# A two-layer hybrid mixer step: GpSimd's element-wise work given to VectorE, and a list schedule made in rounds

## The chip, the core and the metric

The kernel runs on one core of a Trainium2 chip. A core has five engines that run side by side: TensorE (PE, matrix products into PSUM), VectorE (DVE, element-wise work and reductions), ScalarE (ACT, activations and copies), GpSimd (POOL, element-wise work on SBUF here) and SyncE (SP), which in this kernel issues all DMA transfers. Each engine takes its instructions in order; between engines they wait on semaphores. The metric is the device time of one execution in microseconds. TensorE's clock is granted by the chip, at 2.4 GHz or 1.2 GHz; profile rows give the granted share.

## What is computed

Two layers with separate weights run over 128 prompt tokens and 512 latent tokens (640 together, width 1024). In each layer:

```python
mod = silu(cvec) @ w_mod + b_mod                    # shift, scale, gate
h = rms_norm(x, g_pre) * (1 + scale) + shift
p = h @ w_in                                        # 1024 x 3456
ya = rwkv_branch(...)   # 4 heads of 64, two directions, state scan:
                        # s = s*w + (s @ -kk)(kk*a) + v k ; y = s @ r
yb = window_gqa(...)    # 2-D rope, windowed attention with a sink
yc = rglru_branch(...)  # conv over 4 taps, gated linear recurrence, two directions
yd = diff_attend(...)   # two softmaxes, p1 - lam * p2, 4 heads
y = concat(ya*silu(ag), yb*silu(bg), yc*silu(cg), yd*silu(dg)) @ w_out
x = x + gate * rms_norm(y, g_post)
```

The outputs are both token sets after two layers and the prompt's keys, values and final states.

## The kernel before

Tokens are held as five tiles of 128 (four latent, one prompt). Activations for products are kept as a high and a low part in single-pass float32 (tiles HA and HB), and weights are split the same way, so one projection step is three products (high x high, high x low, low x high). `split` (L519 to L525) makes the high part by a copy (ScalarE, or the engine called `self.G`, L524) and the low part by a subtraction (L525, `self.V` or `self.G`). All matrix products go through one helper, so they carry line L352.

A layer runs like this. Weights come in 512 KB pieces through two `raw` buffers (L536; modulation weights L420), are split into WP or WQ, and feed the input projection: feature-major tiles (`fm`) and token-major chunks (`tm_chunk`). Token-major chunks 2 and 4 get rotary embedding in `rope` (L586 to L591), five small element-wise instructions a tile, on `self.G`; chunks 0 and 1 on `self.V`.

The recurrence branch `lru` (L1002) is a convolution, gates, and scans; its tables LRU_CONV, LRU_Q, LRU_U, LRU_S, LRU_H say which steps use `self.G` (1) or `self.V` (0). `stt` (L990) does a step as one scalar-tensor-tensor instruction on VectorE or as two instructions on `self.G`.

The RWKV branch is blocked: chunks of 64 tokens, and for each of two directions d the stages pre (decays and scaled keys), mats (masked block products, L1210), ends, inv, keys, solve; then a chain over chunks, a readout, and the normalisation `rwkv_out`. `rwkv_inv` (L1251) inverts 80 triangular 32x32 blocks at once: the blocks go through DRAM into a layout with one block a partition (L1262, L1264), then for each of 31 columns j an outer product (L1278) and a subtraction (L1280) of j(32-j) elements. CUT = 24 divides the columns: for direction 0 GpSimd has columns below 24 and VectorE the last 8, for direction 1 the mirror. The result goes back through DRAM (L1282, L1283, then four L1286 and two L1288), and two sets of 40 small products join the 32-blocks to 64-blocks.

Then come the differential attention (`diff_tile`: maximum L878, exponentials L881, combination L885 and L886, values L892 to L906), the remaining gate tiles (L700 to L703), the output projection `out`, and `post` (L1545): square sum (L1556), `rsqrt` by three Newton steps (L366 to L381), scaling (L1561), residual sum on `self.G` (L1562), store (L1563). In layer 0 `post_norm` and `modulate` make the next layer's HA and HB.

What sets the order: the program is first recorded without running (`plan`, L1873), every instruction gets an estimated duration (`_length`), and `_list_schedule` (L1800) places instructions engine by engine: among those that are ready it takes the one with the longest remaining tail of dependent work. It models TensorE's clock (`_Clock`), a cost TURN of 0.1 us for changing between products with at most 64 rows and others, and that VectorE and GpSimd hold each other up on SBUF operands (`port`). `follow` then fixes that order on each engine, the DMA issues on SP too.

Of the kernel before, what the change touches and what calls it, by code (L numbers as in the profile page):

```python
# [103 lines left out]
D_BANKS = (2, 3, 6, 7), (4,)  # L104
CUT = 24
F_WO = (9, 12)
# [5 lines left out]
F_RO = (1, 3, 4, 5, 6)  # L112
LRU_CONV = (0, 1)
LRU_Q = (1, 1, 1, 1)
LRU_U = (0, 1, 0, 1)
LRU_S = (0, 1, 0, 1)
LRU_H = (1, 1)
W_F = 0
# [141 lines left out]
class Net:  # L260
    def __init__(self, tc, es, I, O, dbg=None):
        self.tc, self.nc, self.I, self.O = tc, tc.nc, I, O
        self.dbg = dbg or {}
        nc = tc.nc
        self.V, self.A, self.G, self.P = nc.vector, nc.scalar, nc.gpsimd, nc.tensor
        self.pool = es.enter_context(tc.tile_pool(name="sb", bufs=1))
# [356 lines left out]
    def tm_evac(self, l, ch, i, ps):  # L623
# [30 lines left out]
        elif ch in (2, 4):  # L654
            dst = self.at(self.turn("st", M_ST), [128, 256])
            if i == 4:
                A.activation(dst, ps, AF.Copy)
                if ch == 2:
                    nc.sync.dma_start(O["ndk"][l], dst)
            else:  # L660
                x = self.t1([128, 256])
                A.activation(x, ps, AF.Copy)
                self.rope(self.G, dst, x, i, 8, 32, C_C32, C_S32)
            nc.sync.dma_start(self.qkv[1 if ch == 2 else 0, :, i, :], dst)
# [1063 lines left out]
def _width(a):  # L1728
    return math.prod(k for _, k in list(a.ap)[1:])
# [10 lines left out]
def _operands(i):  # L1740
    return [a for a in i.ins if hasattr(a, "ap") and hasattr(a, "memref")]
# [20 lines left out]


def _shares(i):

    if _engine(i) == "Pool":
        return bool(_operands(i))
    return (_engine(i) == "DVE" and not any(map(_in_psum, (*i.outs, *_operands(i))))
            and type(i).__name__[4:] not in ("Memset", "Reciprocal", "TensorReduce"))


TURN = 0.1
STAY = 2.0
# [24 lines left out]


def _list_schedule(names, engine, length, deps, size, half, port):  # L1800

    succ, left = {n: [] for n in names}, {}
    for n in names:
        left[n] = len(deps[n])
        for x in deps[n]:
            succ[x].append(n)
    seen = lambda n, s: (0.0 if engine[n] == "PE" else SAME) if engine[n] == engine[s] != "SP" else SEEN.get(engine[n], 0.0)
    todo, tail, free = [n for n in names if not left[n]], {}, dict(left)
    for n in todo:
        for s in succ[n]:  # L1810
            free[s] -= 1
            if not free[s]:
                todo.append(s)
    for n in reversed(todo):
        own = length[n] + (2.0 + size[n] / 320 if engine[n] == "SP" else 0.0)
        tail[n] = own + max((tail[s] + seen(n, s) for s in succ[n]), default=0.0)
    rank = {n: (-tail[n], k) for k, n in enumerate(names)}
    queues, turned, held = ENGINES + (None,), False, {"DVE": 0.0, "Pool": 0.0}
    clock = _Clock()
    idle, link, ready = dict.fromkeys(queues, 0.0), 0.0, dict.fromkeys(names, 0.0)  # L1820
# [4 lines left out]
    while len(out) < len(names):  # L1825
# [6 lines left out]
        if e == "PE":  # L1832
            if half[n] != turned:
# [7 lines left out]
                else:  # L1841
                    t += TURN
            turned = half[n]
# [18 lines left out]
        if e == "SP":  # L1862
            link = max(link, t + 1.2) + size[n] / 320
            end = link + 0.6
        for s in succ[n]:
            ready[s] = max(ready[s], end + seen(n, s))
# [3 lines left out]
    return out  # L1870


def plan(I, O):  # L1873
# [72 lines left out]
```

## Time and profile before

| | |
|---|---|
| timed runs (3) | 1174.52, 1188.54, 1189.49 us |
| median | 1188.54 us |
| profiled execution | 1178.09 us, its span 1176.3 us |
| busy PE / DVE / ACT / POOL | 1056.7 / 701.6 / 515.0 / 381.7 us |
| bytes moved by DMA | 99.97 MB, mean 85 GB/s |

Busy time is the union of an engine's instructions. Matrix products overlap in TensorE's pipeline, so its busy share says that something was in it, not that it ran at its own pace. The chain that ended last is followed back from the last instruction through whatever released each step.

### The profile page before, as it was taken

Reading aid. Unit: us, or ns where it says so; the run is one execution under the profiler, and the core shown is the slowest. Engines: PE = TensorE matmul, PEld = TensorE weight load, DVE = VectorE, ACT = ScalarE, POOL = GpSimd, SP = SyncE. Lnnn points to the kernel's source line nnn. Section 1 sums busy time; section 2 is a strip of 40 time slices with the busy share of each in tenths; the row PEclk is TensorE's granted clock in tenths of the full one; section 3 lists DMA queues with packets and bytes.
Section 4 is the critical chain, followed back from the end, with each engine's and each line's share of the span. In section 5 each row is a group of like instructions: output and inputs, shape, how many; then the busy total and the mean of one; then the engine's idle time right before and its main releaser. Section 6 shows DMA issues by size and latency. Waiting matters only on the chain.

```text
span 1176.3 us, 24765 instructions
## 1 busy us (share of the span) xinstructions
PE 1056.7 (90%) x10166; PEld 899.5 (76%) x10166; DVE 701.6 (60%) x1646; ACT 515.0 (44%) x1154; POOL 381.7 (32%) x465
## 2 busy tenths in 40 slices
PE   4999988869988998899997999889997998999996
PEld 2798766758876786677996987688886787777796
DVE  4823477526567569478566248672667656967622
ACT  5426433124243547556226473223424354766410
POOL 0032443505780010015123366450577002112312
PEclk9999989769987999889998999987999899999898
DMA  9421344540323031014312102433031303101311
GB/s 367 163 70 69 120 128 118 178 118 9 86 76 81 7 104 43 19 36 139 109 72 90 55 30 83 113 108 95 13 92 65 81 7 120 45 19 37 126 55 54
DMA packets 60225, 99.97 MB, mean 85 GB/s; under 512 B 30736, under 2 KB 38672, under 8 KB 60112
## 3 DMA queue, kind: packets, MB, share of 16 engines
q1 hardware_dynamic: 60112, 98.39, 26.1%
q8 instruction: 80, 1.31, 0.5%
q14 instruction: 33, 0.27, 0.1%
HBM read 82.90 MB, written 15.47 MB: 84 GB/s over the span
## 4 chain that ended last, share of the span: by engine, by line
PE 62%; DVE 11%; ACT 8%; issue 8%; DMA 7%; POOL 3%; SPq 1%; POOLq 0%; ACTq 0%; DVEq 0%
PE banks L352 55%; PE banks L892 2%; PE banks L848 2%; DMA raw<-in_w_tm 1%; PE banks L783 1%; DMA F<-inv 1%; DMA inv<-F 1%; ACT FA L881 1%; DVE F L1280 1%; DMA raw<-in_w_m 1%; PE banks L1235 1%; POOL F L1562 1%; SPq L1286 1%; DMA inv<-ZA 1%; DVE WP L525 1%
## 5 line engine op out<-in xcount | busy, mean ns | idle before, releaser
L352 PE MATMUL banks<-HA,WP 128*128 128x384 f32 (+1 forms) x768 | 208.5, 339 | 7.7 <-DVE mt L701 5.4
L352 PE MATMUL banks<-WP,HA 128*128 128x256 f32 x880 | 186.8, 300 | 14.2 <-ACT WP L522 10.6
L352 PEld LDWEIGHTS banks<-WP,HA 128*128 128x128 f32 x880 | 145.1, 200 | 27.7 <-ACT WP L522 11.1
L352 PEld LDWEIGHTS banks<-HA,WP 128*128 128x128 f32 x768 | 140.0, 202 | 17.8 <-DVE mt L701 6.3
L352 PE MATMUL banks<-HB,WP 128*128 128x384 f32 (+1 forms) x384 | 126.5, 335 | 1.5 <-DVE rq L367 1.1
L352 PE MATMUL banks<-WP,HB 128*128 128x256 f32 x440 | 119.2, 298 | 0.0
L525 DVE TENSOR_TENSOR WP<-raw,WP 128x1024 fp32r<-128x1024 f32 x44 | 56.4, 1282 | 62.6 <-ACT WP L522 60.5
L352 PEld LDWEIGHTS banks<-WP,HB 128*128 128x128 f32 x440 | 82.8, 200 | 4.1 <-issue 3.3
L352 PEld LDWEIGHTS banks<-HB,WP 128*128 128x128 f32 x384 | 76.5, 201 | 5.2 <-issue 2.1
L352 PE MATMUL banks<-WQ,HA 128*128 128x256 f32 x320 | 77.3, 302 | 2.0 <-DVE WQ L525 0.9
L522 ACT ACTIVATE WP<-raw 128x1024 fp32r<-128x1024 f32 x46 | 48.4, 1059 | 64.4 <-PE banks L352 42.0
L352 PE MATMUL banks<-FA,F 64*128 64x128 f32 (+3 forms) x768 | 66.7, 277 | 5.0 <-DVE FA L1177 2.2
L352 PE MATMUL banks<-F,ZA 64*64 64x64 f32 (+2 forms) x1440 | 62.4, 228 | 5.9 <-DMA F<-inv 5.1
L352 PEld LDWEIGHTS banks<-F,ZA 64*64 64x64 f32 (+2 forms) x1440 | 55.1, 140 | 14.8 <-issue 6.8
L703 POOL TENSOR_TENSOR F<-F,mt 128x256 f32<-128x256 f32 (+1 forms) x16 | 19.2, 1199 | 137.3 <-DVE mt L701 119.8
L352 PEld LDWEIGHTS banks<-WQ,HA 128*128 128x128 f32 x320 | 58.0, 202 | 6.1 <-issue 3.1
L878 DVE TENSOR_REDUCE dm<-banks 128x2 f32<-128x1280 f32 (+1 forms) x40 | 50.9, 1273 | 19.0 <-PE banks L352 18.8
L352 PEld LDWEIGHTS banks<-FA,F 64*128 64x128 f32 (+2 forms) x768 | 47.9, 158 | 17.1 <-issue 7.5
L881 ACT ACTIVATE FA<-banks,dm 128x640 f32<-128x640 f32 (+1 forms) x80 | 56.4, 709 | 8.1 <-DVE dm L878 6.1
L352 PE MATMUL banks<-F 128*64 128x128 f32 (+3 forms) x256 | 44.0, 358 | 5.2 <-ACT F L763 3.8
L352 PE MATMUL banks<-WQ,HB 128*128 128x256 f32 x160 | 47.4, 301 | 0.0
L352 PE MATMUL banks<-HA,WQ 128*128 128x384 f32 (+1 forms) x192 | 45.6, 310 | 0.5 <-ACT K L733 0.5
(340 smaller groups left out, 2637.4 us busy)
## 6 DMA issues: line engine op xcount, KB each, us to landing
raw<-in_w_m SPq DMA_DIRECT2D x32, 512.0 KB, 3.5
raw<-in_w_fm SPq DMA_DIRECT2D x30, 512.0 KB, 3.4
raw<-in_w_tm SPq DMA_DIRECT2D x24, 512.0 KB, 3.7
raw<-in_w_o SPq DMA_DIRECT2D x16, 512.0 KB, 3.4
F<-in_x SPq DMA_DIRECT2D x10, 512.0 KB, 4.3
qkv<-F SPq DMA_DIRECT2D x30, 128.0 KB, 1.8
F<-qkv SPq DMA_DIRECT2D x6, 640.0 KB, 5.7
ZA<-in_w_m SPq DMA_DIRECT2D x6, 512.0 KB, 9.9
```

Source lines behind the costliest of these rows:

```text
L352: self.P.matmul(out, lhsT, rhs, start=start, stop=stop)
L522: self.A.activation(hi, x, AF.Copy)
L525: (E or self.V).tensor_tensor(lo, x, hi.bitcast(F32), op=ALU.subtract)
L703: self.G.tensor_tensor(x, x, g, op=ALU.mult)
L783: P.transpose(pt[:, b * 128:(b + 1) * 128], eh[:, b * 128:(b + 1) * 128], self.ident)
L848: P.transpose(reg[0:96, j * 128:j * 128 + 128], tmp[:, i, m].rearrange("p a d -> p (a d)").bitcast(F32), self.ident)
L878: V.tensor_reduce(nm, sc, axis=AX.X, op=ALU.min)
L881: A.activation(e[:, m, :], sc[:, m, :], AF.Exp, bias=nm[:, m:m + 1], scale=-1.0, accum_out=s1 if m else s0)
L892: P.transpose(ps[:, k:k + 128], e[:, 0, k0 + k:k0 + k + 128], self.ident)
L1235: P.transpose(kt[:, p, m, :], self.KR[d, m][:, 2 * i + p, 0, :], self.ident)
L1280: E.tensor_tensor(N[:, rows, cs], N[:, rows, cs], t, op=ALU.subtract)
L1286: nc.sync.dma_start(blk(p, b, rw), nd[us].rearrange("u s t -> s u t"))
```

## The change

Four things. `self.G`, the handle through which GpSimd's element-wise instructions were written, now is VectorE, so GpSimd keeps only the constants that the program's start sets. CUT = 0 gives the inverse's columns to one instruction in each of its steps, and the LRU tables are all 0, so each `stt` is one instruction. The scheduler makes six rounds: a forward pass as before gives a plan and each instruction's end; a backward pass from the ends, under the engines' limits, gives each instruction's latest time, which is the next round's priority; the plan with the shortest modelled length is kept. And TensorE's products are sorted into four kinds in place of two, with 0.3 us for a change to or from the kind with at most 32 weight columns (the modulation products).

```diff
-CUT = 24
+CUT = 0
-LRU_CONV = (0, 1)
-LRU_Q = (1, 1, 1, 1)
-LRU_U = (0, 1, 0, 1)
-LRU_S = (0, 1, 0, 1)
-LRU_H = (1, 1)
+LRU_CONV = (0, 0)
+LRU_Q = (0, 0, 0, 0)
+LRU_U = (0, 0, 0, 0)
+LRU_S = (0, 0, 0, 0)
+LRU_H = (0, 0)
...
-        self.V, self.A, self.G, self.P = nc.vector, nc.scalar, nc.gpsimd, nc.tensor
+        self.V, self.A, self.G, self.P = nc.vector, nc.scalar, nc.vector, nc.tensor
...
-                self.rope(self.G, dst, x, i, 8, 32, C_C32, C_S32)
+                self.rope(self.V, dst, x, i, 8, 32, C_C32, C_S32)
...
+def _kind(i):
+    m, k = _width(_operands(i)[1]), list(i.ins[0].ap)[0][1]
+    return 1 if k <= 64 else 2 if m <= 32 else 3 if m <= 64 else 0
...
-TURN = 0.1
+TURN = 0.1, 0.3
...
+ROUNDS = 6
...
     for n in reversed(todo):
-        own = length[n] + (2.0 + size[n] / 320 if engine[n] == "SP" else 0.0)
-        tail[n] = own + max((tail[s] + seen(n, s) for s in succ[n]), default=0.0)
...
+        tail[n] = own[n] + max((tail[s] + _seen(engine, n, s) for s in succ[n]), default=0.0)
+    rank, best = {n: -tail[n] for n in names}, None
+    for _ in range(ROUNDS):
+        out, ends = _forward(names, engine, length, deps, succ, size, half, port, {n: (rank[n], k) for k, n in enumerate(names)})
+        if best is None or max(ends.values()) < best[0]:
+            best = max(ends.values()), out
+        rank = _backward(names, engine, length, own, deps, succ, size, ends)
+    return best[1]
+
+def _backward(names, engine, length, own, deps, succ, size, ends):
+    left, ready, late = {n: len(succ[n]) for n in names}, dict.fromkeys(names, 0.0), {}
...
+    while len(late) < len(names):
+        t, k = min((idle[e] if here[e] else max(idle[e], come[e][0][0]), k) for k, e in enumerate(queues) if here[e] or come[e])
+        e = queues[k]
...
+        _, n = heapq.heappop(here[e])
+        end = t + own[n]
+        if e == "SP":
+            link = max(link, t) + size[n] / 320
+            end = link + 2.0
+        if e:
+            idle[e] = t + length[n] + NEXT.get(e, 0.0)
+        late[n] = -end
+        for x in deps[n]:
+            ready[x] = max(ready[x], end + _seen(engine, x, n))
+            left[x] -= 1
+            if not left[x]:
+                heapq.heappush(come[engine[x]], (ready[x], -ends[x], x))
+    return late
...
-                    t += TURN
+                    t += TURN[2 in (half[n], turned)]
...
-    half = {n: engine[n] == "PE" and list(trace[n].ins[0].ap)[0][1] <= 64 for n in names}
+    half = {n: engine[n] == "PE" and _kind(trace[n]) for n in names}
```

What this does to the order is shown at three places. The first is SP, the queue of DMA issues, in layer 0 from the loads during the first inverse to its way back. `raw<-in_w_m` are halves of modulation chunks, `raw<-in_w_tm` halves of a token-major projection chunk, `inv<-F` the inverse going to DRAM, `ZA<-inv` its return. Before (four more `in_w_m` and two `in_w_tm` halves stand ahead of these rows, behind the load of the inverse's input):

```order
L420 DMA raw_2107<-in_w_m 128x1024
L668 DMA qkv_89<-F_77 128x256
L420 DMA raw_2113<-in_w_m 128x1024
L668 DMA qkv_89<-F_77 128x256
L420 DMA raw_2153<-in_w_m 128x1024
L420 DMA raw_2159<-in_w_m 128x1024
L420 DMA raw_2199<-in_w_m 128x1024
L668 DMA qkv_89<-F_77 128x256
L420 DMA raw_2205<-in_w_m 128x1024
L668 DMA qkv_89<-F_77 128x256
L1282 DMA inv_67_1229<-F_77 80x1024
L1283 DMA inv_68_1230<-F_77 80x1024
```

```order
L536 DMA raw_2219<-in_w_tm 128x1024
L1286 DMA ZA_79<-inv_67_1229 32x20x32 x4
L1288 DMA F_77<-inv_68_1230 32x20x32 x2
L536 DMA raw_2223<-in_w_tm 128x1024
L536 DMA raw_2377<-in_w_tm 128x1024
```

Now, from the load of the inverse's input on:

```order
L1264 DMA F_77<-inv_66_1219 80x1024
L420 DMA raw_1824<-in_w_m 128x1024
L420 DMA raw_1870<-in_w_m 128x1024
L420 DMA raw_1876<-in_w_m 128x1024
L420 DMA raw_1922<-in_w_m 128x1024
L420 DMA raw_1928<-in_w_m 128x1024
L536 DMA raw_1945<-in_w_tm 128x1024
L536 DMA raw_1949<-in_w_tm 128x1024
L420 DMA raw_2006<-in_w_m 128x1024
L1282 DMA inv_67_1220<-F_77 80x1024
L420 DMA raw_2012<-in_w_m 128x1024
L668 DMA qkv_89<-F_77 128x256
```

The inverse's result leaves behind 8 loads of weights where it left behind 12, and the next token-major chunk (`raw_2219` and `raw_2223` before) no longer has one half ahead of the inverse's return and one behind it: both stand nine and ten rows behind that return.

The second place is PE at the two sets of 40 products that join the inverse's blocks (32x32). `WP` with `HA` or `HB` are projection products, `const,s` the columns of a modulation chunk. Before:

```order
L352 MATMUL banks<-const_66,s_118_2211 128x2 x2
L352 MATMUL banks<-WP_85,HA_83 128x256
L352 MATMUL banks<-F_77,ZA_79 32x32 x40
L352 MATMUL banks<-WP_85,HA_83 128x256
L352 MATMUL banks<-WP_85,HB_84 128x256
L352 MATMUL banks<-WP_85,HA_83 128x256 x2
L352 MATMUL banks<-WP_85,HB_84 128x256
L352 MATMUL banks<-WP_85,HA_83 128x256 x2
L352 MATMUL banks<-ZA_79,F_77 32x32 x37
```

Now:

```order
L352 MATMUL banks<-F_77,ZA_79 32x32 x40
L352 MATMUL banks<-WP_85,HA_83 128x256 x2
L352 MATMUL banks<-WP_85,HB_84 128x256
L352 MATMUL banks<-WP_85,HA_83 128x256 x2
L352 MATMUL banks<-WP_85,HB_84 128x256
L352 MATMUL banks<-WP_85,HA_83 128x256 x2
L352 MATMUL banks<-WP_85,HB_84 128x256
L352 MATMUL banks<-WP_85,HA_83 128x256 x2
L352 MATMUL banks<-WP_85,HB_84 128x256
L352 MATMUL banks<-raw_2052,cs_68 32x256 x4
L352 MATMUL banks<-raw_2058,cs_68 32x256
L352 MATMUL banks<-ZA_79,F_77 32x32 x40
```

Twelve projection products and five of a modulation chunk stand between the two sets, where seven projection products stood; and the products ahead of the first set are from the chunk already loaded, where one product of a new chunk had to come first.

The third place is DVE in the inverse of direction 1, layer 0, around its widest steps. L1278 and L1280 are the inverse (the last size is rows x columns of the step), L755 to L775 window attention, L586 and L590 the rotary embedding of chunk 4, L525 a weight split. Before:

```order
L1278 TENSOR_TENSOR WQ_1999<-WQ_1999,F_77 80x192
L755 TENSOR_REDUCE smw_3522<-banks 128x2
L1280 TENSOR_TENSOR F_77<-F_77,WQ_1999 80x24x8
L757 TENSOR_TENSOR smw_3524<-smw_3522,sink_130_3505 128x2
L1278 TENSOR_TENSOR WQ_1999<-WQ_1999,F_77 80x184
L758 TENSOR_SCALAR smw_3524<-smw_3524 128x2
L1280 TENSOR_TENSOR F_77<-F_77,WQ_1999 80x23x8
L775 TENSOR_TENSOR smw_3517<-smw_3517,smw_3514 128x2
```

Now:

```order
L1278 TENSOR_TENSOR WQ_1944<-WQ_1944,F_77 80x192
L758 TENSOR_SCALAR smw_3410<-smw_3410 128x2
L586 TENSOR_TENSOR F_77<-F_77,const_66 128x256
L1280 TENSOR_TENSOR F_77<-F_77,WQ_1944 80x24x8
L590 TENSOR_TENSOR F_77<-F_77,const_66 128x128
L1278 TENSOR_TENSOR WQ_1944<-WQ_1944,F_77 80x207
L525 TENSOR_TENSOR WP_85<-raw_2326,WP_85 128x1024
L1280 TENSOR_TENSOR F_77<-F_77,WQ_1944 80x23x9
```

The rotary instructions, which GpSimd did, now stand between the halves of the inverse's steps, and the widths go on growing past 192.

## Rows read from the trace of the kernel before

**Rows 1.** Page, part 1: busy us (share of the span) and instructions.

```profile
PE 1056.7 (90%) x10166; PEld 899.5 (76%) x10166; DVE 701.6 (60%) x1646; ACT 515.0 (44%) x1154; POOL 381.7 (32%) x465
```

**Rows 2.** Page, part 4: the chain that ended last, by engine, by line.

```profile
PE 62%; DVE 11%; ACT 8%; issue 8%; DMA 7%; POOL 3%; SPq 1%; POOLq 0%; ACTq 0%; DVEq 0%
PE banks L352 55%; PE banks L892 2%; PE banks L848 2%; DMA raw<-in_w_tm 1%; PE banks L783 1%; DMA F<-inv 1%; DMA inv<-F 1%; ACT FA L881 1%; DVE F L1280 1%; DMA raw<-in_w_m 1%; PE banks L1235 1%; POOL F L1562 1%; SPq L1286 1%; DMA inv<-ZA 1%; DVE WP L525 1%
```

**Rows 3.** Span (us) and mean granted TensorE clock.

```profile
core 0: 1176.3 us, clock 0.934
```

**Rows 4.** Stretches: length, busy time (and instructions) by engine, clock, DMA share, GB/s.

```profile
240.00:270.00 30.00, 21.70 (x519) 19.46 (x521) 7.93 (x15) 10.80 (x24) 2.29 (x4) 0.66 0.37 96
317.00:368.00 51.00, 42.58 (x268) 35.30 (x267) 38.96 (x113) 21.42 (x60) 30.69 (x65) 0.83 0.19 57
436.00:543.00 107.00, 96.82 (x641) 76.77 (x641) 79.97 (x146) 67.47 (x176) 20.81 (x13) 0.92 0.12 40
570.00:600.00 30.00, 30.00 (x248) 29.50 (x247) 14.47 (x44) 5.69 (x11) 6.67 (x4) 1.00 0.15 55
992.00:1088.00 96.00, 88.60 (x625) 71.72 (x625) 76.55 (x146) 66.65 (x173) 18.82 (x13) 0.96 0.12 36
```

**Rows 5.** GpSimd's groups: busy us, mean ns of one, idle before.

```profile
L1280 POOL TENSOR_TENSOR F<-F,KPP 80x23 f32<-80x23 f32 (+11 forms) x92 | 41.6, 452 | 5.3
...
L1562 POOL TENSOR_TENSOR F<-F 128x1024 f32<-128x1024 f32 x10 | 24.8, 2477 | 63.0 <-DVE F L1561 46.6 <-DVE rq L366 11.9 <-issue 4.4
...
L1278 POOL TENSOR_TENSOR KPP<-F 80x23 f32<-80x23 f32 (+11 forms) x46 | 22.3, 485 | 17.0 <-DMA F<-inv 13.9
L1278 POOL TENSOR_TENSOR KPP<-WQ,F 80x23 f32<-80x23 f32 (+11 forms) x46 | 19.8, 431 | 5.6 <-DMA WQ<-inv 3.6
```

**Rows 6.** VectorE's groups, same columns.

```profile
L525 DVE TENSOR_TENSOR WP<-raw,WP 128x1024 fp32r<-128x1024 f32 x44 | 56.4, 1282 | 62.6 <-ACT WP L522 60.5 <-PE banks L352 2.0
...
L886 DVE SCALAR_TENSOR_TENSOR FA<-FA,dm 128x640 f32<-128x640 f32 (+1 forms) x40 | 33.9, 851 | 1.2
...
L1278 DVE TENSOR_TENSOR WQ<-WQ,F 80x112 f32<-80x112 f32 (+29 forms) x62 | 21.8, 352 | 16.9 <-DMA WQ<-inv 16.2
...
L1190 DVE SCALAR_TENSOR_TENSOR ZA<-ZA,K 128x640 f32<-128x640 f32 x8 | 12.3, 1542 | 0.0
```

**Rows 7.** VectorE in time, first inverse: start, length, instruction, idle before.

```profile
225.23 0.22 DVE L441 TENSOR_SCALAR gadd<-banks,par 128x2 f32<-128x2 f32 x1 [3.91 <-PE banks L352]
...
225.69 0.26 DVE L1278 TENSOR_TENSOR F<-F 80x112 f32<-80x112 f32 x1
...
233.02 0.22 DVE L441 TENSOR_SCALAR gadd<-banks,par 128x2 f32<-128x2 f32 x1 [3.95 <-PE banks L352]
...
236.59 0.16 DVE L1280 TENSOR_TENSOR F<-F 80x8 f32<-80x8 f32 x1
```

**Rows 8.** VectorE in time, end of layer 1's attention.

```profile
1104.56 0.17 DVE L376 TENSOR_TENSOR rq<-rq 128x10 f32<-128x10 f32 x1
...
1106.79 2.31 DVE L376 TENSOR_TENSOR rq<-rq 128x10 f32<-128x10 f32 x1
```

**Rows 9.** GpSimd in time, the same stretch.

```profile
1106.66 2.42 POOL L525 TENSOR_TENSOR ZA<-raw,ZA 128x1024 fp32r<-128x1024 f32 x1 [4.64 <-ACT ZA L522]
```

**Rows 10.** PE's waits: us in total, times, longest us.

```profile
PE banks L492 <- DVE s L381: 12.6, 1, 12.6
PE banks L352 <- ACT WP L522: 10.6, 3, 7.8
PE banks L352 <- DVE mt L701: 5.4, 2, 3.5
```

**Rows 11.** PE in time, where the first inverse of layer 0 returns.

```profile
246.19 0.58 PE L352 MATMUL banks<-WP,HA 128*128 128x256 f32 x1 [7.83 <-ACT WP L522]
```

More of the change, by code (lines that the diff above doesn't have):

```diff
@@ L1797, in run, with _seen @@
             self.k, self.busy = self.k + 1, 0.0
+ROUNDS = 6
+def _seen(engine, n, s):
+    return (0.0 if engine[n] == "PE" else SAME) if engine[n] == engine[s] != "SP" else SEEN.get(engine[n], 0.0)
 def _list_schedule(names, engine, length, deps, size, half, port):
-    succ, left = {n: [] for n in names}, {}
+    succ = {n: [] for n in names}
     for n in names:
-        left[n] = len(deps[n])
         for x in deps[n]:
             succ[x].append(n)
-    seen = lambda n, s: (0.0 if engine[n] == "PE" else SAME) if engine[n] == engine[s] != "SP" else SEEN.get(engine[n], 0.0)
@@ L1808, in _list_schedule @@
-    todo, tail, free = [n for n in names if not left[n]], {}, dict(left)
+    left = {n: len(deps[n]) for n in names}
+    todo, tail = [n for n in names if not left[n]], {}
     for n in todo:
         for s in succ[n]:
-            free[s] -= 1
-            if not free[s]:
+            left[s] -= 1
+            if not left[s]:
                 todo.append(s)
+    own = {n: length[n] + (2.0 + size[n] / 320 if engine[n] == "SP" else 0.0) for n in names}
     for n in reversed(todo):
-        own = length[n] + (2.0 + size[n] / 320 if engine[n] == "SP" else 0.0)
-        tail[n] = own + max((tail[s] + seen(n, s) for s in succ[n]), default=0.0)
@@ L1817, in _list_schedule @@
-    rank = {n: (-tail[n], k) for k, n in enumerate(names)}
-    queues, turned, held = ENGINES + (None,), False, {"DVE": 0.0, "Pool": 0.0}
-    clock = _Clock()
+        tail[n] = own[n] + max((tail[s] + _seen(engine, n, s) for s in succ[n]), default=0.0)
[5 more added lines that the diff above has]
+        rank = _backward(names, engine, length, own, deps, succ, size, ends)
@@ new lines, in _list_schedule @@
+    return best[1]
+def _backward(names, engine, length, own, deps, succ, size, ends):
+    left, ready, late = {n: len(succ[n]) for n in names}, dict.fromkeys(names, 0.0), {}
+    queues = ENGINES + (None,)
+    idle, link = dict.fromkeys(queues, 0.0), 0.0
+    come, here = {e: [] for e in queues}, {e: [] for e in queues}
+    for n in names:
+        if not left[n]:
+            heapq.heappush(come[engine[n]], (0.0, -ends[n], n))
+    while len(late) < len(names):
+        t, k = min((idle[e] if here[e] else max(idle[e], come[e][0][0]), k) for k, e in enumerate(queues) if here[e] or come[e])
+        e = queues[k]
+        while come[e] and come[e][0][0] <= t:
+            _, r, n = heapq.heappop(come[e])
+            heapq.heappush(here[e], (r, n))
+        _, n = heapq.heappop(here[e])
[12 more added lines that the diff above has]
+    return late
@@ L1820, in _list_schedule, with _forward @@
+def _forward(names, engine, length, deps, succ, size, half, port, rank):
+    left = {n: len(deps[n]) for n in names}
+    queues, turned, held = ENGINES + (None,), 0, {"DVE": 0.0, "Pool": 0.0}
+    clock, ends = _Clock(), {}
     idle, link, ready = dict.fromkeys(queues, 0.0), 0.0, dict.fromkeys(names, 0.0)
@@ L1864, in _list_schedule @@
             end = link + 0.6
+        ends[n] = end
         for s in succ[n]:
-            ready[s] = max(ready[s], end + seen(n, s))
+            ready[s] = max(ready[s], end + _seen(engine, n, s))
             left[s] -= 1
@@ L1869, in _list_schedule @@
                 heapq.heappush(come[engine[s]], (ready[s], rank[s], s))
-    return out
+    return out, ends
 def plan(I, O):
```

## The prediction

> **What bounds the kernel now.** I read the busy times first [rows 1]: TensorE (PE) is busy 1056.7 us of 1176.3 (90%), VectorE (DVE) 701.6 (60%), GpSimd (POOL) 381.7 (32%). PE looks like the bound, but its spans overlap in a pipeline, so I went on to the chain that ended last [rows 2]: 62% of the span is PE, 11% DVE, 3% POOL; the rest is ScalarE, DMA and issue time. So about a third of the span hangs on something else than PE, and a change of the other engines can be seen. The third view is the clock: its mean is 0.934 [rows 3]. It has two levels, 2.4 GHz and 1.2 GHz, so the lower one was granted for 0.066/0.5 = 13% of the span, 155 us, which costs 78 us at most. The stretches [rows 4] show where. From 570 to 600 us PE never pauses and the clock is full: there nothing but PE counts. From 240 to 270 us, where the first blocked inverse of the layer comes back, PE is busy 21.7 of 30 us and the mean clock is 0.66. In the two attention stretches (436 to 543 and 992 to 1088 us) DVE is busy 80.0 of 107 and 76.6 of 96 us, the fullest of the long ones.
>
> The sum below is made against the profiled execution, 1178.09 us (1.8 us lie outside its span). It stands 0.9% below the median of the three timed runs, 1188.54, and 0.3% above their lowest.
>
> **A. GpSimd's steps that lie on the chain.** POOL's 3% of the chain are 35 us. Some 10 of them are the residual sums of L1562 [rows 2], nearly all under PE's last products; of these only the very last, 2.4 us, ends the kernel. That leaves 27 us that count. A GpSimd instruction with two inputs of 128x1024 takes 2477 ns (L1562) [rows 5], the DVE one of this width 1282 ns (L525) [rows 6]: a factor of 0.52. Saved: 27 x 0.48 = 13 us. If such a step must queue on DVE it saves less (part C); the bounds are 0 and 27.
>
> **B. DVE's own instructions that GpSimd delays.** Side by side with a 2.42 us GpSimd instruction [rows 9], a ten-column L376 took 2.31 us; the same instruction a little earlier took 0.17 [rows 8]. It stands in the serial normalisation ahead of the last output product. L1190 averages 1542 ns, L886, same operation and width, 851 [rows 6]: 8 x 0.69 = 5.5 us. In the inverse, 248 DVE instructions (four groups of 62, one of them in rows 6) average about 0.35 us at a mean width near 102 (j x min(8, 32-j) columns in step j, 3156 over 31 steps); when GpSimd's half was done, 112 columns took 0.26 us and 8 columns 0.16 [rows 7], so 102 should take 0.25, and 248 x 0.1 = 25 us are delay. These show 33 us; I put 40 for the kernel. DVE's part of the chain is 11% of 1176 = 129 us of 701.6, or 18%. 18% of 40 is 7; with the 2.1 us seen directly I take 8. The lower bound is 2, the upper one 40.
>
> The Trainium skill ("SBUF — State Buffer", "Who interferes with whom") says that VectorE and GpSimd share one pair of ports under an exclusive lock, and that a VectorE instruction with two SBUF inputs beside a GpSimd instruction that reads SBUF waits for the whole of it, or the reverse. The 2.31 us above agree. Taken for all work that lies side by side, the rule makes B 21 us instead of 8 and the sum 1126 instead of 1139; the third rival works this out from rows.
>
> **The inverse costs nothing more.** With CUT = 0 one DVE instruction covers all columns: widths j(32-j), 5456 over 31 steps, mean 176 in place of 102. The slope of the two lone rows above is 0.96 ns a column, so 0.32 us each and with their 0.03 us spacing 62 x 0.35 = 22 us an inverse; now DVE's half alone costs 62 x 0.35 = 21.8 [rows 6]. GpSimd's half (41.6 + 22.3 + 19.8 = 83.7 us in all [rows 5]) simply vanishes. Bounds from nothing gained to 1 us lost per inverse.
>
> **C. What is added to DVE.** The rest of GpSimd's work, 381.7 - 83.7 = 298 us, times 0.52 is 155 us. DVE then has 702 - 40 + 155 = 817 us, 69% of the span. By stretch [rows 4], with GpSimd's work there at 0.52: 91 of 107, 86 of 96, and in the second inverse (317 to 368), GpSimd's 30.7 less 21 of inverse, 44 of 51. Nothing overflows, but three such stretches stand at 85 to 90%. DVE runs its queue in order, so a moved instruction delays what is behind it: the row order shown for DVE puts rotary steps between two halves of an inverse step. At the lower bound all of it fits DVE's idle time: 0. At the upper bound it hits the chain as an average DVE instruction does, 18% of 155 = 28. I take 10, nearer to the lower end, because the schedule ranks what ends late first. The fused recurrence steps and the memsets are inside these 155 us.
>
> **D. The new order.** Its largest visible piece is the first inverse of layer 0. In the trace PE waits 7.83 us for a weight split [rows 10, 11]: the weights' second half is queued on SP behind the four write-backs of the inverse, which wait for their data. After it the clock is low: 0.66 in 240 to 270 us means 20 us at 1.2 GHz, 10 us lost at most. On DVE two evacuations of modulation chunks (L441) hold the inverse 3.91 and 3.95 us [rows 7], since they wait for PE and PE for a load. In the new SP order the inverse's result leaves after 8 weight loads instead of 12, and both weight halves of the chunk on PE stand ahead of it; on PE 12 products of it lie between the two block products instead of 7. So I expect most of 7.83 + 10 back: 12 us. The bounds are 0 and 18.
>
> What the six rounds find elsewhere no row shows. PE's idle time is 120 us, of which 12.6 are the first loads [rows 10], some 10 the tail (an estimate) and 8 the hole above: 89 remain, and of the clock's loss 68. The bounds are 0 and 157, and a small loss where the planner's durations are off. Behind the first two entries of the list of waits the third totals only 5.4 us, so no single place holds much; I take a tenth, 16 us. Grouping PE's kinds by TURN costs or gives nothing by itself; it is inside this.
>
> **Sum.** 1178 - 13 (A) - 8 (B) + 10 (C) - 12 - 16 (D) = 1139 us, 3.3% below the profiled execution and 4.2% below the median.
>
> **Rivals.**
> *Nothing comes through*: the chain is 62% PE, and where a DVE or GpSimd step gets shorter PE's own pace (as in 570 to 600 us) or a DMA takes over. Then only the tail's 1.2 us and a little of D stay: about 1175. For it speaks that most waits of PE are short; against it the clock, which PE at its own pace would hold.
> *DVE becomes the queue that everyone waits in* (the slower side): in the attention stretches DVE's idle time of 27 and 19 us is itself waiting for PE and ScalarE and cannot be filled. The four full stretches (two attention, two second inverses, layer 1's taken like layer 0's) grow by the moved work, 11 + 10 + 5 + 5 = 31 us, and a quarter of the other 124 us lands on the path, 31 us; with A and B gained, 1178 + 31 + 31 - 21 = 1219. It decides if DVE cannot pass about 85% in those stretches. Against it: those stretches are not the chain's DVE pieces alone, PE holds much of them.
> *The delay beside GpSimd is larger than its rows show*: DVE is busy 60% of the time, so 229 of GpSimd's 381.7 us lie beside DVE work; if half of that blocks, 115 us are delay, 18% of it 21 us, not 8: 1126. The Trainium skill's port rule (same page and section) points here.
> *The order is worth more*: two fifths of the 157 us, 63 in place of 16: 1092.
> *The change does not do what it says*: if the first round's plan wins, the order differs by the new durations alone, and the last term of D is 0: 1155. This lies in the forecast's own range.
>
> **How the numbers follow.** The forecast (1110 to 1165) has 0.40, the larger delay 0.13, the better order 0.10, nothing 0.22, the DVE queue 0.15. The likeliest is 1139. A range of 1090 to 1190 leaves out most of the slow rival and a little of the fast end. About 2% is what a measurement of this kernel can tell from no change; against 1188.5 that is 1165 and 1212. Faster: 0.40 + 0.13 + 0.10, less the forecast's upper edge, 0.60. Same: 0.25. Slower: 0.15.
>
> **What would show it.** A: no POOL instruction but the constants', the tail a microsecond shorter. B: L376, L1190 and the inverse at 0.17, about 0.85 and near 0.33 us. C: DVE busy near 800 us; the attention stretches as long as before. D: no 8 us hole of PE at the first inverse, and a mean clock above 0.95. If PE's list of waits shows DVE longer than before in the attention stretches, C was too small; if the clock stays at 0.93, D was too large.

## The result, and the profile of the changed kernel

The changed kernel takes 1115.24 us (median of four runs, 1108.33 to 1127.48), the kernel before 1189.01 us beside it (1174.52 to 1190.9). The ratio is 0.9385, with a 95% interval of 0.9282 to 0.9488; it leaves out the run of 1127.48 us, which shows the slower state that some executions of any kernel fall into. In a second group of runs it was 0.9428 (0.9365 to 0.9492). The forecast was 1139 us, which is 0.958 of 1188.5; the time lies in the range of 1090 to 1190, and the sign is right. The gain is 69 to 74 us (65 between the two profiled executions) where the sum had 39 against the profiled execution. What is to be explained is thus where some 30 us more came from.

The first view is the changed kernel's page: busy times (part 1), and the chain that ended last by engine (part 4). The third line is its span and mean granted clock.

```profile
PE 1015.8 (91%) x10166; PEld 883.6 (80%) x10166; DVE 755.2 (68%) x1905; ACT 515.9 (46%) x1154; POOL 0.2 (0%) x4
...
PE 59%; DVE 21%; ACT 8%; DMA 7%; issue 3%; SPq 2%; ACTq 0%; DVEq 0%
```

```profile
core 0: 1111.2 us, clock 0.961
```

Against [rows 1 to 3], POOL has four constants left, and DVE is busy 53.6 us more, not the 115 of the forecast. PE is busy 41 us less with the same 10166 products, at a clock of 0.961 for 0.934. The chain's part of DVE grew from 11% to 21%, but it lost POOL's 3% and 5 points of issue time.

The second view is VectorE's groups: busy us, mean ns of one, idle time before. They answer to [rows 6]; L376 answers to [rows 8].

```profile
L525 DVE TENSOR_TENSOR WP<-raw,WP 128x1024 fp32r<-128x1024 f32 x46 | 56.0, 1218 | 36.1 <-ACT WP L522 35.1 <-PE banks L352 0.5 <-DMA par<-in_par 0.4
L886 DVE SCALAR_TENSOR_TENSOR FA<-FA,dm 128x640 f32<-128x640 f32 (+1 forms) x40 | 30.9, 774 | 0.8
...
L1278 DVE TENSOR_TENSOR WQ<-WQ,F 80x31 f32<-80x31 f32 (+15 forms) x62 | 20.6, 332 | 12.2 <-DMA WQ<-inv 11.9
...
L844 DVE SCALAR_TENSOR_TENSOR F<-F 128x160 fp32r<-128x160 f32 x32 | 9.8, 318 | 3.9 <-ACT F L843 3.8
...
L1190 DVE SCALAR_TENSOR_TENSOR ZA<-ZA,K 128x640 f32<-128x640 f32 x8 | 6.6, 820 | 0.0
...
L376 DVE TENSOR_TENSOR rq<-rq 128x20 f32<-128x20 f32 (+1 forms) x24 | 4.1, 172 | 0.6
```

Every one of these runs in less time than before: L1190 820 ns for 1542, L886 774 for 851. Operation and sizes are the same, but for L1278, whose steps became wider (176 columns on average for 102) and still take 332 ns for 352. L844 and L1210, which are not among the rows of before, stood there as follows (same columns, one shape each):

```profile
L1210 DVE TENSOR_TENSOR ZA<-banks,const 128x512 f32<-128x512 f32 x40 | 25.5, 684 | 10.2 <-PE banks L352 10.1
...
L844 DVE SCALAR_TENSOR_TENSOR F<-F 128x160 fp32r<-128x160 f32 x32 | 18.4, 589 | 4.7 <-ACT F L843 4.7
```

L844, which reads SBUF twice, fell from 589 to 318 ns; L1210, one of whose inputs is in PSUM ("banks"), was 684 and is 680. I summed this over the forms that VectorE runs in both kernels, each with its count of before times the change of its mean (the 197 largest groups of each kernel, by shape): 82 us came off VectorE's own instructions, while the moved work added 164. (Successive records overlap, so busy time rose by less than the difference.) Over all forms, the small ones too, it is 89 us. The prediction had put this delay at 40.

The third view is stretches of the changed kernel, with the columns of [rows 4]. They are: the start of the second direction after the first inverse returns, the second inverse of layer 0, the solve behind it, layer 0's attention, layer 1's solve, layer 1's attention.

```profile
213.00:243.00 30.00, 24.15 (x462) 19.74 (x461) 7.04 (x16) 8.59 (x21) 0.00 (x0) 0.77 0.54 145
270.00:324.00 54.00, 51.59 (x392) 46.82 (x391) 45.77 (x144) 18.07 (x44) 0.00 (x0) 1.00 0.38 115
324.00:385.00 61.00, 59.02 (x1008) 48.48 (x1010) 37.81 (x110) 34.65 (x96) 0.00 (x0) 1.00 0.13 33
402.00:499.00 97.00, 92.66 (x705) 78.26 (x705) 81.87 (x163) 68.10 (x175) 0.00 (x0) 0.98 0.15 49
842.00:903.00 61.00, 60.39 (x998) 48.85 (x998) 37.00 (x109) 33.77 (x95) 0.00 (x0) 0.97 0.15 38
921.00:1026.00 105.00, 97.84 (x727) 83.47 (x726) 81.89 (x164) 69.95 (x178) 0.00 (x0) 0.97 0.14 43
```

The corresponding stretches of the kernel before that [rows 4] does not hold (the second inverse from its first matrix to its end, and the solve behind it):

```profile
297.00:367.00 70.00, 61.03 (x433) 52.40 (x430) 46.60 (x130) 24.02 (x66) 43.55 (x83) 0.88 0.26 74
367.00:418.00 51.00, 49.89 (x922) 40.81 (x921) 28.52 (x80) 25.33 (x68) 2.38 (x4) 0.97 0.17 42
```

The second inverse went from 70 to 54 us, and PE waits in it for 2.4 us, not 9. The solve went from 51 to 61 us, but PE is never short of work there (59.02 of 61): it holds 1008 products where it held 922. That is work put there by the order, not a loss. The two attention stretches are 97 and 105 us long for 107 and 96, in sum the same.

### The profile page after: what moved, and what is told of

It is laid out like the page before. It is cut to its first block, busy times and chain, and to the rows that moved or that the text cites. A ratio compares the mean times of both kernels' runs of the same rounds, so it can differ in the third digit from the quotient of the medians.

```text
span 1111.2 us, 24444 instructions
## 1 busy us (share of the span) xinstructions
PE 1015.8 (91%) x10166; PEld 883.6 (80%) x10166; DVE 755.2 (68%) x1905; ACT 515.9 (46%) x1154; POOL 0.2 (0%) x4
## 4 chain that ended last, share of the span: by engine, by line
PE 59%; DVE 21%; ACT 8%; DMA 7%; issue 3%; SPq 2%; ACTq 0%; DVEq 0%
PE banks L352 53%; DMA F<-inv 2%; DVE F L1280 2%; PE banks L892 2%; DVE WP L525 2%; PE banks L783 2%; PE banks L848 1%; DVE dm L878 1%; DVE F L1278 1%; DVE WQ L1278 1%; DMA inv<-ZA 1%; SPq L1286 1%; ACT F L515 1%; DMA inv<-F 1%; DVE ZA L1210 1%
## 5 line engine op out<-in xcount | busy, mean ns | idle before, releaser
L352 PE MATMUL banks<-HA,WP 128*128 128x384 f32 (+1 forms) x768 | 197.0, 331 | 9.8 <-DVE mt L701 6.1
L352 PE MATMUL banks<-WP,HA 128*128 128x256 f32 x880 | 184.0, 298 | 6.0 <-DVE WP L525 4.9
L352 PEld LDWEIGHTS banks<-HA,WP 128*128 128x128 f32 x768 | 135.0, 196 | 19.2 <-DVE mt L701 7.6
L352 PE MATMUL banks<-HB,WP 128*128 128x384 f32 (+1 forms) x384 | 122.8, 328 | 0.7 <-DVE rq L368 0.7
L352 PE MATMUL banks<-WP,HB 128*128 128x256 f32 x440 | 122.0, 293 | 0.0
L525 DVE TENSOR_TENSOR WP<-raw,WP 128x1024 fp32r<-128x1024 f32 x46 | 56.0, 1218 | 36.1 <-ACT WP L522 35.1
L352 PE MATMUL banks<-WQ,HA 128*128 128x256 f32 x320 | 73.7, 294 | 4.9 <-DVE F L1561 2.8
L352 PE MATMUL banks<-FA,F 64*128 64x128 f32 (+3 forms) x768 | 70.2, 289 | 7.4 <-DVE FA L1177 5.4
L352 PEld LDWEIGHTS banks<-FA,F 64*128 64x128 f32 (+2 forms) x768 | 54.4, 170 | 18.0 <-DVE FA L1177 6.3
L352 PE MATMUL banks<-F 128*64 128x128 f32 (+3 forms) x256 | 39.4, 335 | 1.8 <-ACT F L763 1.6
L352 PE MATMUL banks<-K,HA 128*128 128x256 f32 x160 | 40.8, 285 | 0.2 <-ACT K L522 0.2
```

The lines of the kernel that those rows point to most:

```text
L352: self.P.matmul(out, lhsT, rhs, start=start, stop=stop)
L525: (E or self.V).tensor_tensor(lo, x, hi.bitcast(F32), op=ALU.subtract)
```

## The experiments

The theories. **M**: the move of the work carries the gain, because VectorE's own instructions are no longer delayed. **O**: the order carries it, and the move is worth the prediction's A, B and C. **N**: the long durations of before had another cause than GpSimd. **C** (not the prediction's part C): VectorE's longer queue is what holds the changed kernel back.

### The move alone

The changed kernel, with the planner's three edits taken back:

```diff
-    return 1 if k <= 64 else 2 if m <= 32 else 3 if m <= 64 else 0
+    return 1 if k <= 64 else 0
-TURN = 0.1, 0.3
+TURN = 0.1, 0.1
-ROUNDS = 6
+ROUNDS = 1
```

> The changed kernel with the planner of before: one round, two kinds of matmul, one price for a turn. GpSimd's element-wise work is VectorE's, nothing else differs from the kernel before. Theory M (the move carries the gain: about 100 us of delay of VectorE beside GpSimd are gone, and the chain runs through much of it): 1115 to 1140 us, ratio 0.94 to 0.96, VectorE busy near 755 us as in the changed kernel. Theory O (the order carries it, the move is worth the -13 - 8 + 10 = -11 us of the prediction's terms A, B and C): 1165 to 1185 us, ratio 0.98 to 1.00. If the move alone makes VectorE the queue that everyone waits in, above 1190 us.

Measured: 1150.66 us, ratio 0.9739 (0.9644 to 0.9834). That is 31 us (20 to 42) off some 1178, between M and O, and nearly three times the 11 us of A, B and C. By the prediction's own words the fairer figure is 23 us: its rival 1155, the plan of one round, keeps the 12 us of D at the first inverse, and the 31 agree with that within the interval. Its page, part 1:

```profile
PE 1051.9 (91%) x10166; PEld 893.4 (78%) x10166; DVE 759.1 (66%) x1905; ACT 515.4 (45%) x1154; POOL 0.2 (0%) x4
```

The same-form sum is 82 us less than before here too, with the planner of before. So the shorter instructions come from the move, whatever the order. PE's busy time hardly fell (1056.7 to 1051.9): that part of the changed kernel's gain needs the planner.

### The planner alone

The changed kernel's planner with the tables and `self.G` of before (CUT = 24, LRU tables, GpSimd, the rotary of chunk 4).

> The changed kernel's planner (six rounds with backward passes, four kinds of matmul), with the element-wise work back on GpSimd where the kernel before has it. Theory M: 1165 to 1190 us, ratio 0.98 to 1.00. Theory O: 1115 to 1140 us, ratio 0.94 to 0.96. The prediction's term D: -28 us, ratio 0.976. VectorE busy stays near 700 us and GpSimd near 229 us in all of them. If both this kernel and the move alone come near 1160 us, the two parts add.

Measured: 1156.66 us, ratio 0.9828 (0.9764 to 0.9892), 20 us (13 to 28): what M expected, not O. The prediction's D was 28, at the interval's edge. GpSimd was busy 379.5 us; the 229 us of the expectation is the prediction's estimate of what lies beside VectorE. Its page:

```profile
PE 1049.5 (91%) x10166; PEld 902.3 (78%) x10166; DVE 717.8 (62%) x1646; ACT 515.4 (44%) x1154; POOL 379.5 (33%) x465
```

DVE is busy 16 us longer than before with the same 1646 instructions, and the same-form sum is 19 us up. It may be that the better order lays more of VectorE's work beside GpSimd's, and that the delay eats part of what it finds; this is not shown. Multiplied, the two parts give 0.974 x 0.983 = 0.957; together they give 0.9385 and 0.9428. About 17 to 22 us come only when both are there.

### The old kinds, six rounds, with the move

```diff
-    return 1 if k <= 64 else 2 if m <= 32 else 3 if m <= 64 else 0
+    return 1 if k <= 64 else 0
-TURN = 0.1, 0.3
+TURN = 0.1, 0.1
```

> The changed kernel with the two kinds of matmul and the one price of a turn of before, six rounds kept: it tells what the new kinds alone are worth. Both theories: within 1% of the changed kernel (1105 to 1130 us), since the kinds only reorder what is ready on TensorE. If the kinds are what the order's gain is, above 1135 us.

Measured: 1136.15 us, ratio 0.9654 (0.9591 to 0.9718). The changed kernel in the second group has 0.9428 (0.9365 to 0.9492). The intervals do not meet: the kinds, which I had put at nothing by themselves, are worth some 2 to 3% (above 1135 us, as expected if the order's gain is theirs).

### The changed kernel again, and one round with the new kinds

```diff
-ROUNDS = 6
+ROUNDS = 1
```

> The changed kernel itself, unaltered, beside the other runs of this group on one chip. Move alone (0.974), rounds with the old kinds and the move (0.965) and the planner alone (0.983) were timed in another group than the changed kernel (0.9385). If the parts add, the changed kernel is near 0.974 x 0.983 = 0.957 here, and the 0.9385 belongs to its group; if they help one another, it stays at 0.93 to 0.945.

> The changed kernel with one round in place of six (four kinds of matmul and both prices of a turn kept). With the old kinds one round gave 0.974 and six gave 0.965, and with the new kinds six gave 0.9385. If the kinds carry the gain by themselves, 0.945 to 0.955; if kinds and rounds work only together, 0.965 to 0.98.

Measured: the changed kernel 1108.64 us, 0.9428 (0.9365 to 0.9492); with one round 1124.56 us, 0.9576 (0.9525 to 0.9627). The changed kernel stays in the range for parts that help one another; the one-round kernel lies between its two expectations. So on the moved work the kinds alone take the ratio from 0.974 to 0.958, and the rounds take it on to 0.943. With the old kinds the six rounds were not told apart from one (0.9654 against 0.9739, intervals that overlap). What the kinds do on PE shows in the busy time of the one-round kernel, 1024.3 against 1051.9 us above:

```profile
PE 1024.3 (91%) x10166; PEld 886.8 (79%) x10166; DVE 756.7 (67%) x1905; ACT 514.1 (46%) x1154; POOL 0.2 (0%) x4
```

### The rounds alone, on the kernel before

The planner-alone kernel with the old kinds as well: of the whole change only the six rounds are left.

> The kernel before with six rounds in place of one, and nothing else: two kinds of matmul, element-wise work on GpSimd as before. With the new kinds too this was 0.983. If the rounds carry that, 0.98 to 0.99; if the kinds carry it (on the changed kernel they were worth 0.9406 against 0.9654, 2.5%), 0.995 to 1.01. If it is below 0.975, the new kinds cost time while GpSimd works.

Measured: 1170.59 us, ratio 0.9868 (0.9804 to 0.9931), 16 us: what was expected if the rounds carry the gain there. With the new kinds it was 0.9828: where GpSimd works, the kinds add nothing that can be told apart, while on the moved work they are worth 1.6 to 2.3%.

### The inverse alone

```diff
-CUT = 24
+CUT = 0
```

> The kernel before with the one number that gives the inverse's update wholly to VectorE; ropes, LRU and residual sums stay on GpSimd, and the planner is that of before. Prediction: nothing (the inverse on one instruction a step costs what it costs on two engines, 22 us each of VectorE's own time), ratio 0.99 to 1.01. Theory M in its strong form (the delay sits in the inverse, whose span from first to last step was 39 to 50 us before and 30 to 35 us after): 20 to 40 us off, ratio 0.965 to 0.985, with spans of 30 to 36 us.

Measured: 1185.04 us, ratio 1.0075 (1.0039 to 1.0111): a little slower, as good as nothing. Its page:

```profile
PE 1070.5 (91%) x10166; PEld 907.2 (77%) x10166; DVE 704.3 (60%) x1646; ACT 514.5 (44%) x1154; POOL 298.5 (25%) x281
```

POOL lost 83 us, and DVE, which took them over, has 704.3 us for 701.6. VectorE's own steps of an inverse (with the copy of L1281 behind them) take 22.9, 25.4, 22.1 and 24.9 us, the forecast's 22 in the two that have GpSimd nearly idle beside them (2 us). The two first inverses run in 29 and 32 us from first to last step (39 and 40 before), the two second ones in 52 and 52 (50 and 48): there 20 us of the rotary embedding on GpSimd (L586 to L591) now lie beside them. M in its strong form is wrong: a shorter first inverse is no gain by itself. The next rows are the stretches from layer 0's first mask product (L1210) to that of the second direction, and from there to layer 1's, in the kernel before and in this one:

```profile
180.80:297.40 116.60, 99.61 (x1284) 83.07 (x1281) 65.08 (x153) 36.13 (x75) 47.85 (x73) 0.85 0.37 108
297.40:737.70 440.30, 404.85 (x3590) 347.33 (x3590) 278.74 (x607) 215.03 (x497) 146.91 (x163) 0.95 0.21 69
```

```profile
182.80:287.30 104.50, 87.92 (x1163) 69.77 (x1163) 63.41 (x156) 32.55 (x70) 20.84 (x18) 0.82 0.37 108
287.30:742.40 455.10, 424.81 (x3708) 366.07 (x3707) 279.22 (x611) 218.23 (x501) 133.03 (x125) 0.94 0.21 69
```

The first stretch lost 12 us and some 120 of PE's products, and the second, which has those products now, became 15 us longer.

### GpSimd reading, and GpSimd writing, beside the changed kernel

Both add work that nobody uses to the changed kernel, at the start of each layer, and leave the order on the other engines alone (the lines are shortened here):

```diff
+            for _ in range(230):
+                nc.gpsimd.tensor_tensor(x, self.c[:, 0:256], self.c[:, 256:512], op=ALU.mult)
```

```diff
+            for _ in range(450):
+                nc.gpsimd.memset(x, 0.0)
```

> The changed kernel, with work added that nobody needs: 230 GpSimd products of two 128x256 pieces of the constants at the start of each layer, into a piece of memory that the layer uses only from its first inverse on. The orders of the other engines stay as they are. The rest of each layer is the control within the run. Theory M (VectorE's own instructions take longer beside a GpSimd that reads SBUF: before, about 72 us of excess beside 382 us of busy GpSimd, 0.19 us for one): two stretches of 140 to 170 us of GpSimd make VectorE's busy time 50 to 65 us longer there and nowhere else, and the kernel 12 to 35 us slower (chain share 0.21 to 0.5). Theory N (the durations of before had other causes): VectorE busy within 8 us of the changed kernel's 755, time within 1%.

> The same as the kernel with added products, but GpSimd only writes: 450 fills of 128x256 with zero at the start of each layer, read by nobody. If what delays VectorE is GpSimd's reading (the Trainium skill, SBUF - State Buffer, Who interferes with whom, names the reading and not the writing one), VectorE's busy time stays within 8 us of the changed kernel's and the time within 1%. If any GpSimd access delays VectorE, it is longer by 20 to 60 us, as with the products.

Measured: with the products 1208.77 us (0.9428 became 1.0281, 1.0224 to 1.0338): 100 us lost, and slower than the kernel before. With the fills 1113.91 us, 0.9493 (0.9408 to 0.9577): the same as without. The pages, products first:

```profile
PE 1053.7 (87%) x10166; PEld 911.7 (75%) x10166; DVE 887.2 (73%) x1905; ACT 515.4 (43%) x1154; POOL 441.0 (37%) x464
```

```profile
PE 1017.5 (92%) x10166; PEld 884.9 (80%) x10166; DVE 758.5 (68%) x1905; ACT 515.2 (46%) x1154; POOL 294.5 (27%) x904
```

VectorE needs 132 us more for the same 1905 instructions beside the products, and 3 us more beside the fills. M has the cause of the long durations right, and N is out. The size was far off: 0.40 us of delay for one of GpSimd alone (460 products at 722 ns, the shortest of them, are 332 us; they took 441, so GpSimd is held up too). No engine waits for GpSimd in the list of waits, so the 100 us come through VectorE. Here 100 of 132 us, 76%, reached the end. Part of that is the clock: its mean went from 0.950 to 0.917, which is worth at most 44 us. In the products' second stretch the forms that have a row in the changed kernel's groups as well, by operand, ran as follows (my sums): 24 instructions with an input in PSUM took 19.2 us for 19.4; 231 element-wise ones and scans from SBUF took 174 us for 117, or 0.25 us more each. First that stretch, one row a shape; below it the same shapes in the undisturbed changed kernel, whole span:

```profile
L373 DVE SCALAR_TENSOR_TENSOR rq<-rq 128x1 f32<-128x1 f32 x30 | 16.4, 545 | 0.8
...
L525 DVE TENSOR_TENSOR WQ<-raw,WQ 128x1024 fp32r<-128x1024 f32 x5 | 8.0, 1602 | 0.0
...
L878 DVE TENSOR_REDUCE dm<-banks 128x2 f32<-128x1280 f32 x4 | 5.9, 1480 | 0.5 <-PE banks L352 0.5
...
L376 DVE TENSOR_TENSOR rq<-rq 128x10 f32<-128x10 f32 x3 | 1.5, 494 | 0.1
...
L701 DVE SCALAR_TENSOR_TENSOR mt<-mt,banks 128x384 f32<-128x384 f32 x2 | 1.1, 542 | 0.0
```

```profile
L878 DVE TENSOR_REDUCE dm<-banks 128x2 f32<-128x1280 f32 x32 | 47.6, 1487 | 9.0 <-PE banks L352 8.9
...
L373 DVE SCALAR_TENSOR_TENSOR rq<-rq 128x1 f32<-128x1 f32 x60 | 13.1, 218 | 1.9
...
L701 DVE SCALAR_TENSOR_TENSOR mt<-mt,banks 128x384 f32<-128x384 f32 x8 | 4.4, 547 | 0.0
...
L376 DVE TENSOR_TENSOR rq<-rq 128x10 f32<-128x10 f32 x12 | 2.0, 169 | 0.3
```

One column costs 327 ns more (L373), ten cost 325 (L376), and 1024 cost 385 (L525 WQ, 1217 in the changed kernel). So the price is a wait that does not grow with the instruction's size. The timeline of the products kernel shows the wait: start, length, instruction.

```profile
575.80 0.71 DVE L376 TENSOR_TENSOR rq<-rq 128x10 f32<-128x10 f32 x1
576.55 0.17 DVE L381 SCALAR_TENSOR_TENSOR rq<-rq 128x10 f32<-128x10 f32 x1
576.75 0.60 DVE L375 TENSOR_TENSOR rq<-rq 128x10 f32<-128x10 f32 x1
577.39 0.17 DVE L376 TENSOR_TENSOR rq<-rq 128x10 f32<-128x10 f32 x1
577.59 0.60 DVE L381 SCALAR_TENSOR_TENSOR rq<-rq 128x10 f32<-128x10 f32 x1
```

Every second instruction pays 0.43 to 0.54 us, and the one behind it runs free: the engines take turns. The wait stays below the length of one product here (0.72 us), as the 2.31 us of L376 stayed below its GpSimd neighbour's 2.42 [rows 8, 9]. The Trainium skill ("SBUF — State Buffer", "Who interferes with whom") has this as an exclusive lock on a shared pair of ports, which a VectorE instruction with two SBUF inputs needs only against a GpSimd instruction that reads. Products, fills, and the forms with a PSUM input all agree with it. A form with one input, L524 at 128x512, is held too, 640 ns for 424; the same section of the Trainium skill names its kind (tensor_scalar) among those that can take both pairs of ports.

### More rounds, and the fills back on GpSimd

```diff
-ROUNDS = 6
+ROUNDS = 24
```

> The changed kernel with 24 rounds in place of six: the planner keeps the best of 24 orders by its own estimate. If that estimate follows the chip, 1 to 10 us faster than the changed kernel (0.93 to 0.94); if the rounds have given what they can, within 0.5% of it on either side (0.936 to 0.946); if the estimate is blind to what the chip waits for, slower (0.946 to 0.96).

```diff
-        G.memset(N, 0.0)
+        self.nc.gpsimd.memset(N, 0.0)
```

(and so for the other fills)

> The changed kernel with its fills alone (20 of them, 7.8 us of VectorE) on GpSimd, which reads nothing for them. Since 450 fills at the start of each layer left VectorE's busy time at 758 and the time within 1%, theory M: VectorE busy 747 to 750, no delay in return, kernel 0 to 5 us faster than the changed one (0.935 to 0.943). If the fills' extra hand-over between engines costs more than the freed time, up to 1% slower.

Measured: 24 rounds 1108.18 us, 0.9358 (0.9293 to 0.9424); fills on GpSimd 1108.74 us, 0.9344 (0.9290 to 0.9399). Both medians are among the lowest seen, neither can be told from the changed kernel. The fills behave on VectorE as expected, or slightly better: 745.8 us busy, where it was 755 and 747 to 750 was expected.

```profile
PE 1021.7 (93%) x10166; PEld 887.6 (80%) x10166; DVE 745.8 (68%) x1888; ACT 513.6 (47%) x1154; POOL 9.0 (1%) x21
```

### An edit that missed its aim

```diff
-LRU_Q = (0, 0, 0, 0)
+LRU_Q = (1, 1, 1, 1)
```

(and so for the other four LRU tables)

> The changed kernel with the LRU's share (convolution, gates, state products: about 57 us of GpSimd by the rows of before) back on GpSimd; all else stays on VectorE. It tells whether VectorE's longer queue in the solve (61 us after the second inverse, 51 before) is what gives gain back there. Theory M: VectorE sheds about 25 to 30 us of its own work and takes 0.26 to 0.30 us of delay per GpSimd microsecond, 15 to 17 us, so its busy time falls by only 10 to 15 us to 740 to 745, the delay lands in the second inverses, and the kernel is 5 to 20 us slower (0.945 to 0.96). Theory C (the queue is what is left): the solve stretches shorten by 5 us or more each and the kernel is faster than the changed one (below 0.935).

The tables choose `self.G`, and in the changed kernel that name is VectorE, so nothing went to GpSimd: POOL shows 0.2 us. What ran is the changed kernel with 18 more VectorE instructions (the form that GpSimd needs) and another order. It took 1107.57 us, 0.934 (0.9282 to 0.9399), with VectorE busy 761.6 us. It says nothing on theory C, which stays untested. It does show that 6 us more of VectorE's work need not cost time, and that two orders of nearly the same work cannot be told apart here.

## Why the prediction was right, and where it was off

**The sign and the range** held, and the route is the one forecast: GpSimd's steps and the delay beside it go, DVE has room, and the order adds something. The sum was 30 us short. The move with one round gave 31 us where A, B, C and the 12 us of D at the first inverse come to 23. The planner gave 37 to 42 on top of the move (0.9739 to 0.9428 and 0.9385), and 20 alone, where D's last term had 16. So 21 to 26 us of the shortfall are D's last term, and some 8 are the move's. The rival that had the order worth more (63 for 16) pointed the right way.

**A** cannot be measured apart from B. The tail, its one visible place, became 1.2 us shorter, as said (the last residual sum, L1562, takes 1.2 us for 2.3).

**B was mis-sized as a delay.** I took 40 us from the few rows that showed it; the forms add up to 82. L376, L1190 and the inverse came to 0.17, 0.82 and 0.33 us, so the rows I chose were right and the list was too short: L844 alone gave 8.7 us, L1191 5.1, the rotary embedding on VectorE (L591) 6.9. The third rival had the delay nearer (115 us). How much of it reached the end is not measured. I let 18% do so, DVE's mean share of the chain; in the run with added products it was 76%, but those stood at the start of a layer and the delay of before did not. With 82 us and the 18% kept, B would be 17 and the move 32, near the 31 measured; that agrees, and does not show the share.

**The inverse costs nothing more**: right. The whole inverse on VectorE (with L1281) takes 21.6 to 21.9 us in each of the four, where half of it took 22.0, 23.6, 21.3 and 22.3; moved alone it changes the time by +0.75%. The 25 us of delay that I put there were nearly right too: by the widths, at the changed kernel's durations, the half steps of before would take 64 us where they took 85.

**C**: DVE is busy 755 us, not 817, since B was 42 us too small and successive instructions overlap more. The attention stretches are 202 us together, 203 before, with DVE at 82 of 97 and 82 of 105 us. The second inverses, which the slower rival saw full, are 15 and 14 us shorter from first to last step although DVE is at 46 of 54 us in the first of them. That rival is out: a DVE at 85% in a stretch cost nothing that shows there.

**D**, at the place it named, came, but neither the rounds nor the kinds brought it. The 7.83 us hole for a weight split is gone, and so are the two waits of L441 in the inverse (0.24 and 0.18 us for 3.91 and 3.95). PE's list of waits now begins:

```profile
PE banks L492 <- DVE rq L381: 9.0, 1, 9.0
PE banks L352 <- DMA F<-inv: 6.3, 4, 3.0
PE banks L352 <- DVE mt L701: 6.1, 4, 1.7
```

Two runs with the planner of before have lost the hole as well. This is PE's wait for that split (10.6 us, longest 7.8, in [rows 10]) in the move alone, then in the inverse alone:

```profile
PE banks L352 <- ACT WP L522: 1.0, 1, 1.0
```

```profile
PE banks L352 <- ACT WP L522: 1.3, 1, 1.3
```

The stretch from the first mask product of layer 0 to that of the second direction took 116.6 us before and takes 106.8 in the changed kernel, 106.9 with the move alone and 104.5 with the inverse alone. So the 10 us there, where I put 12, come with the inverse on one engine, and the reason I gave (fewer weight loads ahead of the inverse's way back in the new planner's order) is not needed for them; nor is a shorter stretch a gain by itself, as the inverse alone showed. The clock in the stretch behind the inverse is still low, 0.77 for 0.66, with PE busy 24.15 us of 30. The mean clock of 0.961, and 0.950 in the second group's profile, just meets the 0.95 I named.

**Where D fell short** is its last term, and there the sentence that the kinds of matmul cost or give nothing by themselves. On the moved work they are worth 19 us with one round (0.9739 to 0.9576), and 27 to 32 with six. PE is busy 28 and 14 to 25 us less by them for the same products. The lower clock was granted for 135 us of the move-alone kernel, 122 of the one-round kernel with the kinds, 118 of the six-round kernel without and 88 and 112 of the changed one. So 7 of the 28 us at the most come from the clock.

Most of the rest goes with the changes of kind, by counts and not by a run of its own. Sorted by rows and weight columns as `_kind` does, the products in the trace change kind 599 times in the move alone and 492 times with the kinds; with six rounds it is 568 and 492. In the move-alone trace, at full clock and with no idle time between, the next product starts (median) 0.12 us after a product of the widest kind if it is of that kind too, 0.21 to 0.26 us if it is of another, 0.20 to 0.31 us on the way back, and under 0.06 us within the other kinds. By these medians a change costs 0.1 to 0.2 us more than none (an estimate), and 107 changes 11 to 21 of the 28 us. Where GpSimd works, the kinds take away only 33 changes (554 to 521) and 4 us of PE's busy time (1053.8 to 1049.5), so there they have less to give. Why the planner finds fewer to take away there is not settled; the rise of VectorE's delay under the planner alone (19 us) may be part of it.

## What to carry to other kernels

Price work on GpSimd by the VectorE instructions that run beside it, not by its own time: each of them that reads SBUF alone may wait for the rest of the GpSimd instruction under way, so many small steps beside few long ones should lose most (an inference from the wait's independence of size), and busy times hide it, since the wait is counted as VectorE's work. Compare the mean duration of one form in stretches with and without GpSimd before trusting "GpSimd is free here". Fills may stay on GpSimd. After such a move a planner is worth tuning again: its gain on the moved work was twice that on the old one. And count how often TensorE's products change kind before calling their order free.

## What the hardware showed that I had not expected

The delay does not grow with the size of the delayed instruction: 0.33 us on one column and 0.39 on 1024, and 0.25 on average over 231 instructions beside GpSimd products of 0.72 us. It works both ways: those products took 0.96 us on average. Reductions from PSUM (1480 ns for 1487) take no part in it, and GpSimd's 900 fills of 0.33 us each cost VectorE 3 us in all. A fill takes GpSimd hardly longer than VectorE (80 x 1024: 948 and 912 ns), while a two-input sum of 128x1024 takes it twice as long (2477 ns on average beside VectorE's work [rows 5], and 1224 on VectorE).
